# Decoder step on one core: weight splits, two fill pieces and one absorption in another order

## The chip, the cores and the metric

The kernel runs on one core of a Trainium2 chip. The metric is device time in microseconds (us), the median of three runs. In the rows PE is TensorE's matmuls, PEld its weight loads, DVE VectorE, ACT ScalarE, POOL GpSimd and SP SyncE, which issues DMAs.

## What is computed

One inference step of a hybrid decoder with two layers (DEPTH = 2, width 1024) for a prompt of 512 tokens and for 8 samples of one token, which share the weights. Per layer, cut from the reference:

```python
h = RMSNorm(x); z = h @ W_in
# A: gated linear recurrence, 4 heads; B: latent attention, 8 heads, paged cache of 4096;
# C: gated short convolution
x = x + W_out(concat[A (256), B (512), C (256)])
x = x + SwiGLU(RMSNorm(x))          # hidden width 2816 = 22 tiles of 128
```

The arithmetic is float32. A product of two float32 factors is made of three matmuls: each factor is split into a high part, rounded to the engine's fp32r form, and a low part, the difference; the three are high x high, low x high and high x low.

## The kernel before

**Tiles.** Activations lie transposed: `xt[e]`, e = 0 to 7, holds 128 features of all 520 columns (512 prompt and 8 sample tokens), and a column half is 260 wide. A weight tile `wr` of 128 x 1024 comes by DMA; `wh<-wr` on ACT (or a cast on DVE) makes its high part and `wl<-wr,wh` on DVE its low part. For gated weights the names are `wg` and `wu` (raw), `wgh` and `wgl` (parts). All of these are tiles of pool `w`, which has ten slots (NW_SLOTS, L231). A new tile waits until the last reader of the slot's earlier tile is done. The order on each engine is the order of the program text; every engine runs its own queue in order, and a DMA issue stands in the queue of SP or ACT.

**A layer.** First the projections of h (`z_phase`), in the order of the string `ZSEQ` (L69): z0 to z5 are dense products, k0 to k3 and v0 to v3 keys and values, and `A` calls `absorb` (L815). `absorb` multiplies the samples' queries by `wukt` (16 matmuls `qa`) and spreads the rotary part (4 matmuls `bd`), and copies both with DVE (`qabs`, 8 copies `bd`). Its operands `qn` and `qs` are made by POOL, one head after another. `stat` are the matmuls of a norm; they read `sh` and `sl`, the split squares, and behind them come `ra` (DVE), `ry` and `rh` (ACT), `rh` and `kT` (DVE).

Then the mixers, with a loop over the samples' cache chunks. In the last sample's chain PE has little work of its own, and pieces of the first half of the output projection (matmuls `wo`) are laid between its steps: `FILL1` (L59) and `FILL2` say how many pieces at which step. A tile of `wo` has 24 matmuls in pieces of 9, 9 and 6. `mx` is the transposed maximum of the scores, `ml` the low part of the samples' mixed values; half 1 of the projection needs `ml`.

`out_half(1)` (L1531) is the other column half, tiles n = 0 to 7 with e = 7 - n. The first three use weights that were kept, the others the items at+8 to at+12. Within a tile each step of 128 features has its three matmuls (mh x wh, ml x wh, mh x wl) behind each other. After a tile DVE adds it to `xt[e]`, and ACT and DVE make the gain splits `hh`, `hl` and the square `sq` of the tile before.

**Feed-forward network.** `ffn` (L1678) runs a list of jobs: for the hidden tiles 0 to 3 plain ones (`Plain`: gate with `wg`, then up with `wu`, each 48 matmuls), for the others `Seven`, which makes four products out of seven with sums and differences of the operands, and `Down`, which multiplies finished hidden tiles (`fh`, `fl`) by `wd`. `job.load()` issues the DMAs of the gate's and the up half's weights, `prep_all(0)` splits the first, `prep_all(1)` the second. `differences` is a generator of four sets (`re`, `ro`, `t13`, `t24` and their parts) that `Seven` needs; the loop in `ffn` takes two steps of it at each step of a job (L1703), as well as one step of `end_step` (the gate's activation and `fh`, `fl`) and, where due, one `step()` (loads and splits for a later job).

Of the kernel before, what the change touches and what calls it, by code (L numbers as in the profile page):

```python
# [20 lines left out]
S = 512  # L21
# [34 lines left out]
HOFF = (0, 2, 4, 9, 10)  # L56
AOFF = (0, 1, 2, 4, 6, 7, 9)

FILL1 = [1, 1, 1, 1, 1, 1, 0, 1, 1, 0, 1, 1, 1] + [0] * 8 + [0, 1, 0, 1]  # L59
FILL2 = [1, 1, 1, 1, 2, 2, 2]  # L60
LAST = 8
EARLY = 1
# [3 lines left out]
NH = 4  # L66
TFIRST = 7
PREP = 24
ZSEQ = "s Q e1 v0 k0 v1 G0 v2 v3 G1 z2 e0 H k1 z3 k2 A z4 k3 S z5"  # L69
PVW = 2  # L70
PARTS = (3, 3, 3, 3, 3, 3, 4)
PLAIN = (0, 1, 2, 3)
# [156 lines left out]
class Trunk:  # L229
# [1301 lines left out]
    def out_half(self, half):  # L1531
        at = self.at[self.l]['out']
        if half == 0:
            self.ahead = 1
            self.early = EARLY0
            self.limit = at + 16 - KEEP
            self.w_queue = self.nc.scalar
            self.w_dma(at)
            self.w_dma(at + 1)
            self.acts = [(self.t("mh", F32R), self.t("ml", F32R)) for _ in range(8)]  # L1540
            self.kept = {}
            for k in (6, 7, 0, 1, 2, 3, 4, 5):
                c = slice(0, S if 2 <= k < 6 else T)
                self.split(self.acts[k][0][:, c], self.acts[k][1][:, c], self.mixed[k][:, c])
                yield
                if k == 0:
                    self.w_split(at)
                    self.w_dma(at + 2)
                if k == 4:
                    self.w_split(at + 1)  # L1550
            self.prepared = True
            yield
        else:
            self.ahead = AH2
            self.w_queue = self.nc.sync
            self.early = 1
            self.jobs = self.ffn_jobs()
            self.h2 = [None] * 8
            for k in range(2, 6):
                self.split(self.acts[k][0][:, S:T], self.acts[k][1][:, S:T], self.mixed[k][:, S:T])  # L1560
            self.w_split(at + 8)
            self.w_hi(at + 9)
        c = slice(half * CH, (half + 1) * CH)
        for n in range(8):
            e = 7 - n if half else n
            b = self.ps("wo")
            wt = self.kept.pop(e) if half and n < KEEP else self.w_get(at + 8 + n - KEEP if half else at + n)
            if half:
                self.dense(wt, self.acts, 0, 8, {half: b}, 8, (half,))
            else:  # L1570
                for k0, nk in ((0, 3), (3, 3), (6, 2)):
                    self.dense([x[:, k0 * P:(k0 + nk) * P] for x in wt], self.acts, k0, nk, {half: b}, 8, (half,))
                    if k0 < 6:
                        yield
                if n >= 8 - KEEP:
                    self.kept[e] = wt
            del wt
            if half and n:
                self.h2[e + 1] = self.gain_split(e + 1, G_FFN)
                self.square_in(e + 1)  # L1580
            self.tt(self.xt[e][:, c], self.xt[e][:, c], b[:, 0:CH], ALU.add)
            if half:
                if n == 3:
                    self.jobs[0].load()
                if n == 5:
                    self.jobs[0].prep_all(0)
                if n == 6:
                    self.jobs[1].load()
                    self.jobs[0].prep_all(1)
            yield  # L1590
        if half:
            self.h2[0] = self.gain_split(0, G_FFN)
            self.square_in(0)
            self.x_sums()
# [83 lines left out]
    def ffn(self):  # L1678
# [11 lines left out]
        at, loaded = 1, 2  # L1690

        def step():
            nonlocal at, loaded
            at = next(todo, len(jobs))
            while loaded < min(len(jobs), at + 3):
                jobs[loaded].load()
                loaded += 1

        for n, job in enumerate(jobs):
            while at <= n:  # L1700
                step()
            for k, _ in enumerate(job.run()):
                for _ in range(2):  # L1703
                    if extra is not None and self.rstd2 is not None and next(extra, self) is self:
                        extra = None
                self.end_step()
                if at <= n + job.far:
                    step()
                    if job.pace > 1 and at <= n + 1:
                        step()  # L1710
            if not last and len(jobs) - n in (4, 3, 2):
                m = 4 - (len(jobs) - n)
                if m == 0:
                    self.w_dma(nxt)
                    self.w_dma(nxt + 1)
                elif m == 1:
                    self.w_split(nxt)
                    self.w_dma(nxt + 2)
                else:
                    self.w_split(nxt + 1)  # L1720
                    self.w_hi(nxt + 2)
                    self.w_dma(nxt + 3)
            if job.f == FF - 1 and not isinstance(job, Down):
                self.h3 = self.diffs = None
# [290 lines left out]
```

## Time and profile before

| | us |
|---|---|
| median of three runs | 2197.75 (2195.72 to 2198.5) |
| profiled execution, its own time | 2197.29 |
| its span | 2195.2 |
| PE busy in the span | 2147.8 |
| DVE, ACT, POOL busy | 1760.1, 1291.1, 436.6 |
| granted TensorE clock, mean | 0.998 |

Busy time of PE is time with a matmul in its pipeline. The span goes from the first instruction to the last. A row of a timeline has the start and the duration in us; behind it, in brackets, how long the engine stood idle ahead of it and what ended that.

### The profile page before, as it was taken

The numbers are of one execution on the slowest core, as the hardware profiler recorded it, in microseconds if no ns is written. First come the engines' busy times: TensorE is split into PE (matmuls) and PEld (weight loads), VectorE is DVE, ScalarE is ACT, GpSimd is POOL, SyncE is SP. The second block draws the span as 40 slices with busy tenths as digits, with TensorE's granted clock in tenths as the row PEclk, the third lists the DMA queues.
The fourth block names the chain that finished last, engine by engine and source line by source line (L and its number), as shares of the span: only waits on it lengthen the run. The fifth ranks groups of instructions, "written<-read, shape, count | busy, mean of one in ns | idle before, by whom it ended". The sixth has DMA issues, their size and how long they took to land.

```text
span 2195.2 us, 50795 instructions
## 1 busy us (share of the span) xinstructions
PE 2147.8 (98%) x18330; PEld 2013.3 (92%) x18330; DVE 1760.1 (80%) x3673; ACT 1291.1 (59%) x3364; POOL 436.6 (20%) x470
## 2 busy tenths in 40 slices
PE   8999999999999999999999999999999999999999
PEld 8998888888888999999999988888888889999999
DVE  7778889877676699889777788897776857998895
ACT  6667767677674554444356677676776745444341
POOL 0004334333362000000001134234333610000000
PEclk9999999999999999999999999999999999999999
DMA  5213445453574423333233134445445733333232
GB/s 183 99 49 107 116 129 146 129 148 119 165 227 142 136 84 106 106 110 98 77 103 105 59 96 138 124 134 151 135 130 163 237 120 117 110 106 102 90 104 78
DMA packets 149484, 267.72 MB, mean 122 GB/s; under 512 B 22833, under 2 KB 103090, under 8 KB 149234
## 3 DMA queue, kind: packets, MB, share of 16 engines
q1 hardware_dynamic: 121778, 178.47, 25.7%
q0 software_dynamic: 24576, 75.52, 11.9%
q10 hardware_dynamic: 2880, 10.49, 1.5%
q8 instruction: 145, 2.38, 0.4%
q14 instruction: 105, 0.86, 0.1%
HBM read 259.86 MB, written 4.54 MB: 120 GB/s over the span
## 4 chain that ended last, share of the span: by engine, by line
PE 77%; DVE 12%; ACT 7%; issue 3%; DMA 1%; SPq 0%; POOL 0%; DVEq 0%; POOLq 0%; ACTq 0%
PE k L268 29%; PE b L268 17%; PE pr L268 17%; PE pv L268 3%; PE wo L268 3%; ACT ry L283 2%; PE sc L268 2%; DVE ss L1449 1%; DVE wl L271 1%; PE ov L268 1%; DVE ctl L271 1%; PE gr L268 1%; DVE sl L271 1%; ACT wh L283 1%; DVE z L271 1%
## 5 line engine op out<-in xcount | busy, mean ns | idle before, releaser
L268 PE MATMUL k<-wkh,cth 128*128 128x256 f32 (+1 forms) x2048 | 619.7, 303 | 3.4 <-ACT ksq L283 1.9
L268 PE MATMUL k<-wkh,ctl 128*128 128x256 f32 (+1 forms) x2048 | 581.5, 284 | 7.4 <-DVE ctl L271 7.3
L268 PE MATMUL k<-wkl,cth 128*128 128x256 f32 (+1 forms) x2048 | 578.0, 282 | 0.0
L283 ACT ACTIVATE ksq<-k 128x256 f32<-128x256 f32 x1024 | 378.8, 388 | 273.2 <-PE k L268 269.3
L1449 DVE TENSOR_REDUCE ss<-ksq 128x8 f32<-128x512 f32 x512 | 347.6, 681 | 169.4 <-ACT ksq L283 165.9
L268 PEld LDWEIGHTS k<-wkh,cth 128*128 128x128 f32 x2048 | 385.8, 188 | 54.9 <-ACT s L283 27.4
L268 PEld LDWEIGHTS k<-wkh,ctl 128*128 128x128 f32 x2048 | 385.3, 188 | 12.6 <-DVE ctl L271 11.8
L268 PEld LDWEIGHTS k<-wkl,cth 128*128 128x128 f32 x2048 | 386.1, 189 | 6.5 <-issue 3.8
L1335 POOL DMA_INDIRECT nat<-in_cn,idx x224 | 231.2, 1032 | 517.7 <-PE pv L268 389.9
L268 PE MATMUL b<-fh,wd 128*128 128x260 f32 x1408 | 232.0, 282 | 1.1 <-ACT fh L283 1.1
L271 DVE TENSOR_TENSOR ctl<-ct,cth 128x512 fp32r<-128x512 f32 x256 | 175.8, 687 | 27.4 <-ACT cth L283 26.8
L268 PEld LDWEIGHTS b<-fh,wd 128*128 128x128 f32 x1408 | 195.3, 188 | 1.5 <-ACT fh L283 1.5
L283 ACT ACTIVATE swh<-sw 128x512 fp32r<-128x512 f32 x144 | 90.8, 631 | 133.6 <-DVE sw L271 129.7
L283 ACT ACTIVATE cth<-ct 128x512 fp32r<-128x512 f32 x256 | 163.2, 637 | 1.2 <-DMA ct<-in_ct 1.1
L268 PE MATMUL b<-fl,wd 128*128 128x260 f32 x704 | 141.8, 283 | 0.5 <-DVE fl L271 0.5
L1314 POOL DMA_INDIRECT kr<-in_krt,idx x128 | 132.4, 1034 | 38.6 <-issue 36.4
L268 PE MATMUL b<-hh,wh 128*128 128x260 f32 x640 | 130.7, 285 | 8.0 <-ACT wh L283 7.2
L268 PE MATMUL b<-hl,wh 128*128 128x260 f32 x640 | 130.1, 285 | 0.2 <-DVE hl L274 0.2
L268 PE MATMUL b<-hh,wl 128*128 128x260 f32 x640 | 129.8, 284 | 0.0
L271 DVE TENSOR_TENSOR x<-x,b 128x260 f32<-128x260 f32 x224 | 84.8, 420 | 33.5 <-PE b L268 32.4
L268 PEld LDWEIGHTS b<-fl,wd 128*128 128x128 f32 x704 | 108.4, 188 | 0.9 <-DVE fl L271 0.9
L268 PEld LDWEIGHTS b<-hh,wh 128*128 128x128 f32 x640 | 99.7, 190 | 8.7 <-ACT wh L283 7.2
(346 smaller groups left out, 5209.2 us busy)
## 6 DMA issues: line engine op xcount, KB each, us to landing
ct<-in_ct SPq DMA_DIRECT2D x512, 128.0 KB
wg<-in_w_gate SPq DMA_DIRECT2D x44, 512.0 KB
wu<-in_w_up SPq DMA_DIRECT2D x44, 512.0 KB
wr<-in_w_in SPq DMA_DIRECT2D x40, 512.0 KB
wdr<-in_w_down SPq DMA_DIRECT2D x96, 192.0 KB
wr<-in_w_out ACTq DMA_DIRECT2D x20, 512.0 KB
wdr<-in_w_down SPq DMA_DIRECT2D x16, 256.0 KB
nat<-in_cn,idx POOLq DMA_INDIRECT x224, 3.5
```

Of the source, the lines that this page charges most:

```text
L268: self.nc.tensor.matmul(out, lhsT, rhs, start=start, stop=stop)
L271: (e or self.nc.vector).tensor_tensor(out=out, in0=a, in1=b, op=op)
L283: self.nc.scalar.activation(out=out, in_=a, func=f, **k)
L1314: nc.gpsimd.indirect_dma_start(out=k[:, gq * P:(gq + 1) * P], out_offset=None, in_=a['krt'].rearrange("l n c -> (l n) c"), in_offset=bass. ...
L1335: nc.gpsimd.indirect_dma_start(out=nat(b, i)[:, 0:512], out_offset=None, in_=a['cn'].rearrange("l n c -> (l n) c"), in_offset=bass.Indirec ...
L1449: nc.vector.tensor_reduce(out=ss[:, 8 * t:8 * t + 8], in_=sq[:, 0:512].rearrange("p (h d) -> p h d", d=64), axis=AX.X, op=ALU.add)
```

## The change

Four edits. `FILL1` lays two more fill pieces ahead of `mx`, in the fifth and sixth step, and the later pieces move up by as many. `ZSEQ` has `A` between v3 and G1, before z2, and no more behind k2. `out_half(1)` starts with job 0's loads; of the projection's own items it loads at+8 there (it is already split) and takes the high part of at+9 at n = 1; job 0's first weight is split at n = 1 and its second at n = 3, job 1's loads are issued at n = 4 and its first weight is split at n = 6. In `ffn` the steps of `end_step` and `step()` stand ahead of the two steps of `differences`; a branch for jobs of another pace is gone.

```diff
--- before.py
+++ after.py
@@ -56,7 +56,7 @@
 HOFF = (0, 2, 4, 9, 10)
 AOFF = (0, 1, 2, 4, 6, 7, 9)
 
-FILL1 = [1, 1, 1, 1, 1, 1, 0, 1, 1, 0, 1, 1, 1] + [0] * 8 + [0, 1, 0, 1]
+FILL1 = [1, 1, 1, 1, 2, 2, 0, 1, 1, 0, 1, 1, 1] + [0] * 8 + [0, 1, 0, 1]
 FILL2 = [1, 1, 1, 1, 2, 2, 2]
 LAST = 8
 EARLY = 1
@@ -66,7 +66,7 @@
 NH = 4
 TFIRST = 7
 PREP = 24
-ZSEQ = "s Q e1 v0 k0 v1 G0 v2 v3 G1 z2 e0 H k1 z3 k2 A z4 k3 S z5"
+ZSEQ = "s Q e1 v0 k0 v1 G0 v2 v3 A G1 z2 e0 H k1 z3 k2 z4 k3 S z5"
 PVW = 2
 PARTS = (3, 3, 3, 3, 3, 3, 4)
 PLAIN = (0, 1, 2, 3)
@@ -1558,8 +1558,8 @@
             self.h2 = [None] * 8
             for k in range(2, 6):
                 self.split(self.acts[k][0][:, S:T], self.acts[k][1][:, S:T], self.mixed[k][:, S:T])
-            self.w_split(at + 8)
-            self.w_hi(at + 9)
+            self.w_dma(at + 8)
+            self.jobs[0].load()
         c = slice(half * CH, (half + 1) * CH)
         for n in range(8):
             e = 7 - n if half else n
@@ -1580,13 +1580,17 @@
                 self.square_in(e + 1)
             self.tt(self.xt[e][:, c], self.xt[e][:, c], b[:, 0:CH], ALU.add)
             if half:
+                if n == 0:
+                    self.w_split(at + 8)
+                if n == 1:
+                    self.jobs[0].prep_all(0)
+                    self.w_hi(at + 9)
                 if n == 3:
-                    self.jobs[0].load()
-                if n == 5:
-                    self.jobs[0].prep_all(0)
+                    self.jobs[0].prep_all(1)
+                if n == 4:
+                    self.jobs[1].load()
                 if n == 6:
-                    self.jobs[1].load()
-                    self.jobs[0].prep_all(1)
+                    self.jobs[1].prep_all(0)
             yield
         if half:
             self.h2[0] = self.gain_split(0, G_FFN)
@@ -1700,14 +1704,12 @@
             while at <= n:
                 step()
             for k, _ in enumerate(job.run()):
+                self.end_step()
+                if at <= n + job.far:
+                    step()
                 for _ in range(2):
                     if extra is not None and self.rstd2 is not None and next(extra, self) is self:
                         extra = None
-                self.end_step()
-                if at <= n + job.far:
-                    step()
-                    if job.pace > 1 and at <= n + 1:
-                        step()
             if not last and len(jobs) - n in (4, 3, 2):
                 m = 4 - (len(jobs) - n)
                 if m == 0:
```

SP's queue at half 1 of layer 0, before. `wr` are the items at+10, at+11 and at+12 of the output projection, `wg` and `wu` gated weights of job 0, then of job 1.

```order
L374 DMA wr_12995<-in_w_out 128x1024
L374 DMA wr_13001<-in_w_out 128x1024
L374 DMA wr_13005<-in_w_out 128x1024
L1773 DMA wg_13039<-in_w_gate 128x1024
L1773 DMA wu_13040<-in_w_up 128x1024
L1773 DMA wg_13152<-in_w_gate 128x1024
L1773 DMA wu_13153<-in_w_up 128x1024
```

After:

```order
L1775 DMA wg_12900<-in_w_gate 128x1024
L1775 DMA wu_12901<-in_w_up 128x1024
L374 DMA wr_13003<-in_w_out 128x1024
L374 DMA wr_13009<-in_w_out 128x1024
L374 DMA wr_13013<-in_w_out 128x1024
L1775 DMA wg_13088<-in_w_gate 128x1024
L1775 DMA wu_13089<-in_w_up 128x1024
```

Job 0's two loads stand ahead of the three items of the projection now, and their slots with them.

DVE in the same half before, from the first part of x6's row on (`x_81` is x6, `x_80` x5); `wl` are the low parts for tiles 6 and 7.

```order
L274 SCALAR_TENSOR_TENSOR hl_13032<-x_81,gains_74,hh_13031 128x520
L271 TENSOR_TENSOR sq_12989<-sq_12989,sq_13035 128x520
L271 TENSOR_TENSOR x_80<-x_80,wo_12992 128x260
L271 TENSOR_TENSOR wl_13044<-wr_13001,wh_13003 128x1024
L274 SCALAR_TENSOR_TENSOR hl_13073<-x_80,gains_74,hh_13072 128x520
L271 TENSOR_TENSOR sq_12957<-sq_12957,sq_13076 128x520
L271 TENSOR_TENSOR x_79<-x_79,wo_13043 128x260
L271 TENSOR_TENSOR wl_13081<-wr_13005,wh_13046 128x1024
```

After:

```order
L274 SCALAR_TENSOR_TENSOR hl_13040<-x_81,gains_74,hh_13039 128x520
L271 TENSOR_TENSOR sq_12997<-sq_12997,sq_13043 128x520
L271 TENSOR_TENSOR x_80<-x_80,wo_13000 128x260
L271 TENSOR_TENSOR wgl_13049<-wu_12901,wgh_13047 128x1024
L271 TENSOR_TENSOR wl_13052<-wr_13009,wh_13011 128x1024
L274 SCALAR_TENSOR_TENSOR hl_13081<-x_80,gains_74,hh_13080 128x520
L271 TENSOR_TENSOR sq_12959<-sq_12959,sq_13084 128x520
L271 TENSOR_TENSOR x_79<-x_79,wo_13051 128x260
L271 TENSOR_TENSOR wl_13093<-wr_13013,wh_13054 128x1024
```

A `wgl` of job 0 stands ahead of the `wl` of tile 6; before, that `wl` came right behind the add to x5.

DVE in the projections of layer 0 behind v3, before: `wl` and `wh` are weights of z2 and of the next products.

```order
L271 TENSOR_TENSOR wl_1750<-wr_1548,wh_1620 128x1024
L387 CAST wh_1752<-wr_1622 128x1024
L271 TENSOR_TENSOR sl_1786<-sq_1780,sh_1785 128x520
L271 TENSOR_TENSOR wl_1825<-wr_1622,wh_1752 128x1024
L387 CAST wh_1827<-wr_1754 128x1024
L271 TENSOR_TENSOR z_1879<-b_324_1823,rstd_362 128x260
```

After:

```order
L271 TENSOR_TENSOR wl_1750<-wr_1548,wh_1620 128x1024
L387 CAST wh_1752<-wr_1622 128x1024
L271 TENSOR_TENSOR sl_1786<-sq_1780,sh_1785 128x520
L824 COPY qabs_1820<-qa_1821 128x128
L833 COPY bd_1732<-bd_1831 32x8x4 x8
L271 TENSOR_TENSOR wl_1847<-wr_1622,wh_1752 128x1024
L387 CAST wh_1849<-wr_1754 128x1024
L271 TENSOR_TENSOR z_1901<-b_327_1845,rstd_362 128x260
```

The copies of `absorb` stand behind `sl` here; before, they stood behind a later `sl`, that of k2.

## Rows read from the trace of the kernel before

**Rows 1.** The page, part 1: busy time, share of the span, instructions.
```profile
PE 2147.8 (98%) x18330; PEld 2013.3 (92%) x18330; DVE 1760.1 (80%) x3673; ACT 1291.1 (59%) x3364; POOL 436.6 (20%) x470
```

**Rows 2.** PE's waits: engine, line, releaser: us in total, times, longest us.
```profile
PE b L268 <- DVE wgl L271: 3.8, 2, 1.9
```

**Rows 3.** Stretches, layer 0: length; busy us PE, PEld, DVE, ACT, POOL; clock; DMA.
```profile
763.70:767.11 3.41, 3.41 (x18) 3.41 (x17) 3.41 (x7) 2.71 (x4) 0.00 (x0) 0.50 0.10 18
767.12:770.53 3.41, 3.41 (x31) 3.41 (x30) 3.41 (x7) 0.44 (x1) 0.00 (x0) 1.00 0.11 39
757.79:794.25 36.46, 34.56 (x275) 34.25 (x274) 36.31 (x67) 19.09 (x29) 0.00 (x0) 0.95 0.14 41
800.00:850.00 50.00, 50.00 (x419) 50.00 (x418) 49.71 (x114) 23.38 (x41) 0.00 (x0) 1.00 0.33 106
171.40:174.80 3.40, 3.40 (x27) 3.32 (x27) 1.95 (x6) 1.69 (x4) 2.79 (x3) 1.00 0.69 204
```

**Rows 4.** Timeline, feed-forward network: start, duration, engine, instruction, idle before and its releaser.
```profile
754.63 1.06 ACT L283 ACTIVATE wgh<-wu 128x1024 fp32r<-128x1024 f32 x1 [3.90 <-issue]
...
755.59 0.83 ACT L283 ACTIVATE ry<-stat,consts 128x260 f32<-128x260 f32 x2
...
762.89 0.51 PE L268 MATMUL b<-hh,wgl 128*128 128x260 f32 x2 [1.90 <-DVE wgl L271]
...
794.98 0.51 PE L268 MATMUL b<-fh,wd 128*128 128x260 f32 x2 [0.61 <-ACT fh L283]
```

**Rows 5.** Timeline of PE, last chain of layer 0's samples and half 1.
```profile
695.43 0.27 PE L1365 MATMUL mx<-consts,m 128*8 128x128 f32 x1 [1.30 <-DVE m L271]
...
720.17 0.38 PE L268 MATMUL wo<-ml,wh 128*128 128x260 f32 x1 [0.43 <-DVE ml L271]
```

**Rows 6.** Timeline of DVE, the same stretch.
```profile
716.07 0.43 DVE L271 TENSOR_TENSOR x<-x,wo 128x260 f32<-128x260 f32 x1 [1.16 <-PE wo L268]
```

**Rows 7.** Timeline of POOL, PE and DVE, projections of layer 0.
```profile
137.84 1.16 POOL L278 TENSOR_SCALAR qn<-ev,gains 64x8 f32<-64x8 f32 x1
...
153.97 1.85 PE L268 MATMUL qa<-qn,wukt 128*128 128x16 f32 x16
...
156.12 0.48 PE L268 MATMUL b<-hh,wh 128*128 128x260 f32 x2
...
160.12 0.69 DVE L271 TENSOR_TENSOR sl<-sq,sh 128x520 fp32r<-128x520 f32 x1
...
160.94 1.20 DVE L833 COPY bd<-bd 32x32 f32<-32x32 f32 x8
...
162.07 0.28 PE L268 MATMUL stat<-sl,mats 128*128 128x260 f32 x1
...
171.37 0.39 PE L268 MATMUL stat<-sl,mats 128*128 128x260 f32 x1 [1.47 <-DVE sl L271]
```

**Rows 8.** Timeline of PE, SP, ACT and DVE, half 1 of layer 0.
```profile
728.07 0.28 PE L268 MATMUL wo<-mh,wh 128*128 128x260 f32 x1
...
728.19 0.33 SPq L374 DMA_DIRECT2D wr<-in_w_out  x1
...
728.61 2.35 DVE L271 TENSOR_TENSOR wl<-wr,wh 128x1024 fp32r<-128x1024 f32 x2
...
730.95 0.28 PE L268 MATMUL wo<-mh,wh 128*128 128x260 f32 x1
...
731.70 1.06 ACT L283 ACTIVATE wh<-wr 128x1024 fp32r<-128x1024 f32 x1 [3.65 <-DMA wr<-in_w_out]
...
732.67 0.71 ACT L283 ACTIVATE hh<-x,gains 128x520 fp32r<-128x520 f32 x1
...
733.29 0.62 ACT L283 ACTIVATE sq<-x 128x520 f32<-128x520 f32 x1
...
733.42 0.76 DVE L274 SCALAR_TENSOR_TENSOR hl<-x,gains,hh 128x520 fp32r<-128x520 f32 x1 [2.46 <-ACT hh L283]
...
734.10 0.69 DVE L271 TENSOR_TENSOR sq<-sq,sq 128x520 f32<-128x520 f32 x1
```

## The prediction

> **What bounds the kernel now.** I read the page first: of a span of 2195.2 us PE is busy 2147.8 us [rows 1], so 47 us is all that an order can win. PE is the bound; what counts is where it stands still and what ends that. In the list of PE's waits the second factors `wgl` of the gated weights stand with 3.8 us in two waits, one in each layer [rows 2]. The timelines show the place in layer 0, and layer 1 repeats it. The wait of 1.90 costs more than itself: behind it the granted clock is 0.50 for 3.41 us, in which 18 matmuls run where the next 3.41 us hold 31. That is 13 matmuls at 0.12 us, about 1.5 us [rows 3, 4]. And from 757.79 to 794.25 DVE is busy 36.31 of 36.46 us [rows 3]: DVE, not PE, sets when `fh` comes, and PE waits 0.61 for it at 794.98 although it had lost 1.90 and 1.5 us just before [rows 4].
>
> The profiled execution took 2197.29 us, 0.46 below the median of 2197.75. I sum on its rows and add the sum to the median.
>
> **Fill pieces: -1.7 us per layer.** Two more pieces are 18 matmuls of 0.12 us, 2.2 us of work ahead of `mx`, where PE now stands 1.30 us for DVE's `m` [rows 5]. They cover the wait and put `mx` some 0.7 us later. Their weights are needed one piece earlier, and `p` comes at about the time PE asks for it; from there PE has 18 matmuls fewer to do before half 1. So `ml` must come earlier too, or its wait of 0.43 grows [rows 5]. It can: `ra` now stands behind an add that waits for PE's tile [rows 6], and the changed order puts `ra` ahead of it. The add still needs 24 matmuls after `stat`, 2.9 us, and `ml` follows it. I count both waits, 1.30 and 0.43, as gone. If `ml` is late by 0.7 the gain is 1.0; nothing else is there to win, so 1.0 to 1.7.
>
> **Absorption of the queries: +1.2 us per layer.** The 16 `qa` and 4 `bd` matmuls hold PE for 2.15 us, from 153.97 to 156.12, and the copies hold DVE for 1.4 [rows 7]. At the new place, which PE reaches at 138.0, the last pair of `qn` is not there: POOL ends it at 139.0 [rows 7]. PE gets through 6 of the 16 and waits 0.45. At the old place this work was cover. DVE's chain from one `stat` to the next `sl` ended at 160.81, and PE came for it at 162.07: 1.26 us of slack [rows 7]. Without 2.15 us of PE work in that stretch PE comes 0.9 too early. Behind that `sl` DVE goes to `wl`, `z` and `ra` without the copies, so the chain to the next `sl`, for which PE waits 1.47 at 171.37, takes 1.4 us less. Added up: the first `sl` ends 2.6 us later (2.15 moved ahead of it, 0.45 waited), the next one 2.6 - 1.4 = 1.2 later, and PE's `stat` with it. With `qn` in time it would be +0.75; 0 if PE's shift is taken up at once. Bounds 0 to 1.4.
>
> **Half 1 of the output projection: +4.85 us per layer.** PE has no wait here: a tile of 24 matmuls starts every 2.88 us [rows 8]. The change loads job 0's two weights at the start, into two of the ten slots of pool w, and splits the first at n = 1, the second at n = 3. The loads of the last three tiles' weights (at+10 to at+12) stand behind these in SP's queue, and the slots that they take come free one tile later than before: in the built order at+11, the weights of tile 6, waits for the end of tile 3, at+12 for that of tile 4. Let S be the start of tile 4. The load is issued at S + 0.1; the one issued at 728.19 had landed when `wh` began at 731.70, 3.5 us on [rows 8]. So `wh` of tile 6 holds ACT from S + 3.65 to 4.7. Behind it on ACT, in order, stand `hh` (0.71) and `sq` (0.62) of x6 and job 0's second `wgh` (1.04): to S + 5.4, 6.0 and 7.05. DVE, in order, does `hl` of x6 (0.68 from start to start), the sum of `sq` (0.61), an add to x5 (0.35), then job 0's second `wgl`, held by that `wgh` to S + 7.05 and 1.13 long [rows 8], and only then `wl` of tile 6: S + 8.2 to 9.4. PE asks for that `wl` at the third matmul of tile 6, S + 5.75 + 0.25 = 6.0, and waits 3.45 us. The floor of this term is in the slots: `wl` of tile 6 takes the slot that tile 5 leaves at S + 5.7, so even with DVE free PE waits 1.0.
>
> Tile 6 then ends at S + 12.1. `wl` of tile 7 takes a slot that tile 6 leaves and runs 1.22 us from there: PE waits 0.95. By then the gain splits of x4 to x1 are late on DVE, with job 1's first `wgl` now among them, and `hl` of x1 comes about 0.4 us after PE asks for it in the last eighth of job 0's gate. Together 3.45 + 0.95 + 0.4, and 0.05 at tile 5: 4.85. Bounds 2.4 (the two slot waits and 0.4) and 5.5.
>
> **Clock behind that wait: +1.5 us per layer.** The rows show a half clock behind the wait of 1.90 and full clock behind that of 1.47 [rows 3]. A wait of 3.45 is longer than the one that cost the clock, so I count one such stretch. Bounds 0 and 3.0 (two stretches).
>
> **Feed-forward part: -0.55 us per layer, and +1.5 for the clock.** Let U be the end of job 0's second half on PE, 754.6 [rows 4]. Job 1's first factor is split before U and its second right behind it, so the wait of 1.90 and the half clock go, 3.6 us with the restart. But `fh` of the first down job is late next. `ra` now stands behind that `wgl`, so ACT's `ry` starts 1.6 after U, not 0.96 [rows 4]: the chain to `rstd` is 0.6 later. Behind it DVE has one `wgl` of 1.13 less. It runs without a gap there, and weights ahead of differences take no difference out from before this `gt`. So `gt`, and with it `fh`, comes 0.55 earlier after U, while PE, 3.6 us earlier, waits 3.7 us in place of 0.61. By the rows on the clock a half clock follows, and nothing behind takes that loss up: from 800 to 850 PE is busy 50.00 of 50 us [rows 3]. Bounds -1.1 to -0.3, and 0 to 1.5.
>
> **Sum.** Per layer -1.7 + 1.2 + 4.85 + 1.5 - 0.55 + 1.5 = 6.8 us; two layers 13.6; 2197.75 + 13.6 = 2211.
>
> The Trainium skill, DMA: Bandwidth & Descriptors, "Rules for kernel authors", tells authors to issue a DMA early, compute, and wait on its semaphore late, so that the fixed cost is hidden. By that rule job 0's early loads cost nothing, which is the second rival; the row of 3.5 us from issue to use bears it out, but the rule does not count the slot that an early load holds.
>
> **Rivals.** First, the splits in half 1 wait for their slots alone: loads land sooner or DVE catches up, and PE waits 1.0 + 0.95 + 0.4 with no clock lost; `fh` still costs 1.5. Per layer -1.7 + 1.2 + 2.4 - 0.55 + 1.5 = 2.85: 2203.5. For it: the floor follows from the order. Against it: `wgh`, `wgl` and `wl` stand in one line on two engines behind a load of measured length.
>
> Second, half 1 stays free of waits because the early loads fit: -1.7 + 1.2 - 0.55 + 1.5 = 0.45 per layer, 2198.6, no change. Against it: tile 5 must leave its slot before `wl` of tile 6 is written, and PE asks 0.3 us later.
>
> Third, faster: weights ahead of differences let the `gt` of the first down job overtake. If DVE ends it 3.1 us earlier than I count, PE keeps 3.6 us and the clock; with the slot waits alone in half 1 and the absorption at its bound of 0 that is -1.7 + 2.4 - 3.6 = -2.9 per layer, 2192.0. It decides at the point where three operand splits (0.6 each) and one pair of `re` and `ro` (1.35) fall behind that `gt`. Against it: the built order has all four sets of differences begun ahead of it.
>
> Fourth, the change does not do what its pieces say: `ml` follows `mx`, the fill wins nothing, and the forecast grows by 3.4 to 2214.5.
>
> **Chances.** Forecast, with the clock lost at one or both places and the fourth rival in it (2206 to 2217): 0.62. First rival, 2200 to 2206: 0.16. Second: 0.11. Third: 0.11. A difference under about 0.2% (4.4 us) can't be told from no change on this kernel, so faster is below 2193.4 and slower above 2202.1. Slower is the 0.62 and most of the first rival, 0.74; same 0.14, the second and the low end of the first; faster 0.12. The range leaves out the third rival and the far ends: 2198 to 2217.
>
> **What would show it.** Right: PE waits over 2 us for DVE's `wl` at tile 6 of half 1 and about 1 at tile 7; a granted clock of 0.50 behind that; no wait for `wgl`; 3 to 4 us for `fh`; none at `mx`; 0.45 at `qa`, then `stat` waits of about 0.9 and 1.4. Wrong: half 1 without waits, so that my reading of the slots fails, or a wait for `fh` under 1 us, so that DVE was not the bound.

## The result, and the profile after

The changed kernel takes 2214.5 us (median of 6 runs, 2211.9 to 2215.2), the kernel before on the same chip 2197.6. The ratio is 1.0073 with a 95% interval of 1.0063 to 1.0084: slower by 16.9 us in the medians, 2214.5 where 2211 was forecast with a range of 2198 to 2217. The profiled execution has a span of 2211.5 us and an own time of 2213.2.

The page, part 1, of the changed kernel, to be read beside [rows 1]: PE is busy 6.4 us longer, with the same number of matmuls; 20.5 us of its span stand at half clock around its waits (below), where 6.8 stood before. The rest of the longer span is waiting.

```profile
PE 2154.2 (97%) x18330; PEld 2018.5 (91%) x18330; DVE 1760.8 (80%) x3673; ACT 1291.4 (58%) x3364; POOL 435.6 (20%) x470
```

PE's waits in the changed kernel: engine, line, releaser: us in total, times, longest us.

```profile
PE b L268 <- ACT fh L283: 9.8, 2, 4.9
PE wo L268 <- DVE wl L271: 8.0, 5, 3.2
...
PE mx L1365 <- DVE m L271: 1.4, 4, 0.4
```

Before, the wait for `wgl` stood in this list with 3.8 us [rows 2]. It is gone. In its place stand 9.8 us for `fh`, one wait in each layer, where 1.1 stood before, and 8.0 for `wl` in half 1, where no wait was.

The timeline of half 1 in layer 0, SP, ACT, DVE and PE: start, duration, engine, instruction, and in brackets the idle time ahead and its releaser. It answers to [rows 8].

```profile
729.34 0.33 SPq L374 DMA_DIRECT2D wr<-in_w_out  x1
...
732.95 1.06 ACT L283 ACTIVATE wh<-wr 128x1024 fp32r<-128x1024 f32 x1 [1.71 <-DMA wr<-in_w_out]
733.91 0.71 ACT L283 ACTIVATE hh<-x,gains 128x520 fp32r<-128x520 f32 x1
734.53 0.62 ACT L283 ACTIVATE sq<-x 128x520 f32<-128x520 f32 x1
735.06 1.04 ACT L283 ACTIVATE wgh<-wu 128x1024 fp32r<-128x1024 f32 x1
...
736.28 1.22 DVE L271 TENSOR_TENSOR wgl<-wu,wgh 128x1024 fp32r<-128x1024 f32 x1
737.42 1.22 DVE L271 TENSOR_TENSOR wl<-wr,wh 128x1024 fp32r<-128x1024 f32 x1
...
738.69 0.39 PE L268 MATMUL wo<-mh,wl 128*128 128x260 f32 x1 [2.99 <-DVE wl L271]
...
744.32 0.39 PE L268 MATMUL wo<-mh,wl 128*128 128x260 f32 x1 [0.97 <-DVE wl L271]
```

This is the line that the prediction wrote down: the load for tile 6 is issued at 729.34, its `wh` starts 3.61 us later, `hh`, `sq` and `wgh` of job 0 stand behind it on ACT, `wgl` and only then `wl` on DVE. PE stands 2.99 us in tile 6 and 0.97 in tile 7.

Stretches of the changed kernel, as in [rows 3]: length; busy us of PE, PEld, DVE, ACT, POOL; granted clock; DMA share and GB/s.

```profile
739.03:742.45 3.42, 3.42 (x18) 3.42 (x17) 1.23 (x3) 1.25 (x2) 0.00 (x0) 0.50 0.74 272
...
800.48:803.89 3.41, 3.21 (x13) 2.99 (x14) 3.13 (x8) 1.49 (x4) 0.00 (x0) 0.50 0.13 11
1834.72:1841.53 6.81, 5.57 (x24) 5.26 (x24) 3.42 (x5) 1.92 (x4) 0.00 (x0) 0.50 0.42 154
1896.16:1902.97 6.81, 4.49 (x19) 4.26 (x20) 6.30 (x15) 3.26 (x7) 0.00 (x0) 0.50 0.19 58
```

At the `wl` wait and at the `fh` wait TensorE's granted clock falls to 0.50, its level of 1.2 GHz, for 3.41 us in layer 0 and for 6.8 us in layer 1. In layer 1 it falls while PE still stands, 1.2 us before the end of the `wl` wait and 2.3 us before the end of the `fh` wait, so part of each long stretch has no matmul to slow down.

### The profile page after: what moved, and what is told of

Read it like the earlier page. It is cut to its first block, busy times and chain, and to the rows that moved or that the text cites. A ratio compares the mean times of both kernels' runs of the same rounds, so it can differ in the third digit from the quotient of the medians.

```text
span 2211.5 us, 50789 instructions
## 1 busy us (share of the span) xinstructions
PE 2154.2 (97%) x18330; PEld 2018.5 (91%) x18330; DVE 1760.8 (80%) x3673; ACT 1291.4 (58%) x3364; POOL 435.6 (20%) x470
## 5 line engine op out<-in xcount | busy, mean ns | idle before, releaser
L271 DVE TENSOR_TENSOR wl<-wr,wh 128x1024 fp32r<-128x1024 f32 (+1 forms) x84 | 91.5, 1091 | 20.0 <-ACT wh L283 13.5
```

The source lines that it names most:

```text
L271: (e or self.nc.vector).tensor_tensor(out=out, in0=a, in1=b, op=op)
```

## Where the 16 us lie

The table takes the start of the same matmul in both profiles and gives what each stretch grew by, in us; the forecast is for one layer. The stretches run from the last of the mixers' values `v` to the first scores `sc` (absorption), from there to job 0's gate (fill pieces, half 1 and its clock), to the gate's first `stat`, to the end of the `fh` wait, and to the first `v` of the next layer or the last matmul.

| stretch | forecast | layer 0 | layer 1 |
|---|---|---|---|
| absorption | +1.2 | +0.3 | +0.3 |
| fill, half 1, its clock | -1.7 + 4.85 + 1.5 = +4.65 | +4.8 | +6.2 |
| gate to `stat` | 0 | +0.3 | +0.2 |
| `stat` to the end of the `fh` wait | -0.55 | +0.75 | +0.75 |
| behind `fh` | +1.5 | +1.25 | +1.9 |
| sum | +6.8 | +7.5 | +9.2 |

The two layers add up to 16.7 us; the changed kernel's profile reaches the first of these matmuls 0.5 us sooner, and its span is 16.3 us longer. The forecast's 0.4 for `hl` of x1 is counted in the second row and falls into the third. The third row can't be put down to the change: in a second execution of the kernel before (below) the same stretch is 0.4 and 0.2 us longer than in the first.

## The experiments

Three chips were used. The runs with one edit each ran on a chip on which the kernel before takes 2197.5 us; the second weight loaded and split late, one step in the old order, the kernel before once more and the last run on one on which it takes 2197.6. The other four (the second split late, one slot more, weights first, one step of differences) ran on a chip on which it takes 2300.6 us: there PE waits 19 to 28 us for `ksq` in front of `k` in the cache chunks, where it waits 1.9 us in the profile of the kernel before. Of those four only ratios to the kernel before on that chip, and stretches behind the mixers, are used.

### One edit at a time

**The fill pieces alone.**

```diff
-FILL1 = [1, 1, 1, 1, 1, 1, 0, ...
+FILL1 = [1, 1, 1, 1, 2, 2, 0, ...
```

> The kernel before with the two fill pieces alone. Theory (the fill's term stands by itself): PE's wait of 1.30 at mx goes and that of 0.43 at ml falls to 0.2 or less, both layers: 2197.6 - 3.1 = 2194.5, ratio 0.9986. Rival (ml follows mx, and what the fill wins comes back as a wait at ml): no change, 2197.6. In between, a part that comes back inside half 1: 2196.

Measured: 2195.5 us, ratio 0.9991 (0.9982 to 1.0000): -2.0 us, not -3.1. The waits at `mx` and `ml` are as the theory says (1.30 gone, `ml` 0.2). From the last `mx` to job 0's gate PE needs 2.1 us less in layer 0 and 1.7 in layer 1, and `mx` comes 0.7 to 0.8 later, so 1.4 and 1.0 are won at the gate. In layer 0 all of it was given back behind that. The timeline of PE in this run, feed-forward part of layer 0, to be read beside [rows 4]:

```profile
760.88 0.50 PE L268 MATMUL b<-hh,wgl 128*128 128x260 f32 x2 [1.87 <-DVE wgl L271]
...
792.97 0.50 PE L268 MATMUL b<-fh,wd 128*128 128x260 f32 x2 [2.11 <-ACT fh L283]
```

Stretches of the same run, with the granted clock in the column behind POOL:

```profile
760.85:764.26 3.41, 3.38 (x28) 3.38 (x29) 3.41 (x8) 2.52 (x4) 0.00 (x0) 1.00 0.00 0
763.70:767.11 3.41, 3.41 (x31) 3.41 (x31) 3.41 (x6) 1.37 (x2) 0.00 (x0) 1.00 0.20 58
793.84:797.25 3.41, 3.41 (x17) 3.41 (x18) 3.31 (x9) 1.53 (x3) 0.00 (x0) 0.50 0.38 105
```

Behind a `wgl` wait of 1.87 the clock stayed full here. PE therefore came to `fh` 1.5 us sooner, but DVE did not: the `fh` wait is 2.11 instead of 0.61, and the half clock stands behind that wait now. In the kernel before the half clock fell where PE would have had to wait for `fh` in any case, so it cost nothing. Here it costs. At the gate and at the end of the `fh` wait this run is 2.0 us ahead of the kernel before, 0.6 of it from the very start of the profile; at layer 1's first `v` only 0.45 is left. In layer 1 the half clock stands where it did before, and 1.0 us is kept.

**The absorption alone.**

```diff
-ZSEQ = "s Q e1 v0 k0 v1 G0 v2 v3 G1 z2 e0 H k1 z3 k2 A z4 k3 S z5"
+ZSEQ = "s Q e1 v0 k0 v1 G0 v2 v3 A G1 z2 e0 H k1 z3 k2 z4 k3 S z5"
```

> The kernel before with the queries' absorption moved and nothing else. Theory 1 (the prediction's term): a wait of 0.45 at qa for qn, waits of 0.9 and 1.4 at the two stat: +1.2 per layer, 2200.0. Theory 2 (DVE's chain has slack of its own that takes up most of the shift): no wait at qa, stat waits of 0.85 and 1.0, +0.3 per layer, 2198.2.

Measured: 2199.5 us, ratio 1.0009 (1.0000 to 1.0018): +2.0 us. By the total theory 1 is right, by the place it is wrong. No wait at `qa`, `stat` waits of 0.87 and 1.00, and `sc` comes 0.33 later in layer 0 and 0.7 in layer 1. The rest is the same shift of the half clock as above, now in layer 1: there the clock stayed full behind a `wgl` wait of 1.91, and PE's next wait in this run's timeline is

```profile
1884.98 0.51 PE L268 MATMUL b<-fh,wd 128*128 128x260 f32 x2 [2.16 <-ACT fh L283]
```

with a granted clock of 0.50 for 3.41 us from 1886.85 on. A single number that agrees with a theory would have hidden this.

**Half 1 alone** (the whole hunk of `out_half`):

```diff
-            self.w_split(at + 8)
-            self.w_hi(at + 9)
+            self.w_dma(at + 8)
+            self.jobs[0].load()
...
+                if n == 3:
+                    self.jobs[0].prep_all(1)
...
```

> The kernel before with the new half 1 of the output projection (early loads and splits of the gated weights) and nothing else. Theory 1 (this half alone makes the loss, the fh wait behind it too): wl waits of about 3 and 1 us in tiles 6 and 7, one half-clock stretch behind them in layer 0 and two in layer 1, no wgl wait, and fh waits of 4 to 5 us with a half clock: +19 us, 2216.5. Theory 2 (the new order in the feed-forward part makes the fh wait longer): the same wl waits, but fh waits of 3 to 3.7 us: +16 us or less, 2213.5.

Measured: 2211.0 us, ratio 1.0059 (1.0045 to 1.0073): +13.5 us. PE's waits in this run:

```profile
PE b L268 <- ACT fh L283: 8.0, 2, 4.0
PE wo L268 <- DVE wl L271: 7.8, 5, 3.1
```

From the last `mx` to the gate PE needs 7.0 us more in layer 0 and 6.2 in layer 1, clock included; the profiled execution took 2214.2 us, 3.2 above the median of five, with a mean granted clock of 0.995 where the other four have 0.997 or 0.998, so these two figures are at the high end. The `fh` waits are 4.03 and 3.94 us, shorter than the 4.88 of the full change, but longer than the 3 to 3.7 of theory 2, whose time it has. From job 0's `stat` to the end of the `fh` wait this kernel is even 0.3 us faster than the kernel before.

**The feed-forward order alone.**

```diff
+                self.end_step()
+                if at <= n + job.far:
+                    step()
                 for _ in range(2):
...
-                self.end_step()
-                if at <= n + job.far:
-                    step()
...
```

> The kernel before with weights ahead of differences in the feed-forward loop and nothing else. Theory 1 (the order moves nothing that PE waits for): wgl wait 1.9 and fh wait 0.6 as before, 2197.6. Theory 2 (the high parts of differences stand behind weights on ACT, DVE waits for them, and gt comes later): fh wait 1.5 to 2.5 in each layer, +2 to +4 us with the clock kept, 2200 to 2202. Theory 3 (the order was needed for gt to overtake): no fh wait, -1.2, 2196.4.

Measured: 2202.3 us, ratio 1.0021 (1.0012 to 1.0031): +4.85 us. Theory 2 is right that DVE waits for a high part of the differences on ACT; it has the size of the `fh` wait wrong and, as the rows and the run with weights first below show, what stands ahead on ACT. The `wgl` wait is down to 0.2, with this edit alone, and the `fh` wait is 4.75 in both layers, with a half clock of 6.8 us that begins 2.4 and 1.7 us before the wait is over. The timeline of ACT, DVE and PE in this run, layer 0:

```profile
781.84 0.64 ACT L283 ACTIVATE fh<-gt 128x520 fp32r<-128x520 f32 x1 [3.74 <-DVE gt L271]
782.38 0.51 ACT L283 ACTIVATE wd<-wdr 128x384 fp32r<-128x384 f32 x1
782.80 0.62 ACT L283 ACTIVATE t13h<-t 128x520 fp32r<-128x520 f32 x1
...
783.45 0.70 DVE L271 TENSOR_TENSOR t13l<-t,t13h 128x520 fp32r<-128x520 f32 x1 [1.04 <-ACT t13h L283]
...
794.59 0.80 PE L268 MATMUL b<-fh,wd 128*128 128x260 f32 x2 [4.75 <-ACT fh L283]
```

ACT's `fh` of an earlier hidden tile waits for DVE's product `gt`, and `t13h` stands behind it. DVE needs `t13h` next and is idle for 1.04 us, in a stretch where it has no other gap. From job 0's `stat` to the end of the `fh` wait this run takes 45.4 us, the kernel before 44.4, and the same in layer 1. The changed kernel has the same row, at 789.74 and with 1.04 us.

The four edits give -2.0, +2.0, +13.5 and +4.85, in sum +18.3 against +16.9 together: additive within the intervals, which are 2 to 3 us to either side for each run. A sum above the whole would fit that half 1 and the feed-forward order both remove the same `wgl` wait and pay for the same `fh`, but these runs do not show it.

### What makes half 1 wait

**The second split late.**

```diff
-                if n == 3:
-                    self.jobs[0].prep_all(1)
...
                 if n == 6:
+                    self.jobs[0].prep_all(1)
                     self.jobs[1].prep_all(0)
```

> The changed kernel with job 0's second weight split at n = 6, as before, and not at n = 3; its early loads, the first split at n = 1 and job 1's first split stay. Theory 1 (wgh and wgl of that split stand ahead of wl of tile 6, and the slot that the second split takes keeps wl of tile 6 waiting for tile 5): wh of tile 6 ends at S + 4.7, S being the start of tile 4, and wl at S + 5.9, where PE asks at S + 6.0: waits of 0 to 0.3 at tiles 6 and 7, no half clock there; the fh wait of 4.9 stays: 2214.5 - 2 x (4.0 + 1.5 to 3) = 2200.5 to 2203.5. Theory 2 (the late load of tile 6 alone is enough, whatever stands behind it): wl waits of 2 to 3 us stay, 2212 or more.

Measured: 1.0033 (1.0016 to 1.0050) of the kernel before on its chip. Tile 7's wait is gone, tile 6 still waits 2.04 us in layer 0 and 1.62 in layer 1, with the clock full behind both. So neither theory: about half of the wait was the second split. PE now waits 0.8 us for `hh` in job 0's gate, where the changed kernel has no such wait. The timeline of DVE in this run shows what was forgotten:

```profile
783.25 0.76 DVE L274 SCALAR_TENSOR_TENSOR hl<-x,gains,hh 128x520 fp32r<-128x520 f32 x1 [2.35 <-ACT hh L283]
783.93 0.69 DVE L271 TENSOR_TENSOR sq<-sq,sq 128x520 f32<-128x520 f32 x1
784.54 0.42 DVE L271 TENSOR_TENSOR x<-x,wo 128x260 f32<-128x260 f32 x1
784.87 1.22 DVE L271 TENSOR_TENSOR wl<-wr,wh 128x1024 fp32r<-128x1024 f32 x1
```

`wh` of tile 6 was ready at 782.6, but `wl` starts at 784.87. ACT makes `hh` of x6 only behind that late `wh`, and DVE has `hl`, `sq` and the add ahead of `wl`: a late load delays work that has nothing to do with it.

**One slot more.**

```diff
-    NT_SLOTS = 68
-    NW_SLOTS = 10
+    NT_SLOTS = 66
+    NW_SLOTS = 11
```

> The changed kernel with eleven slots for weights instead of ten, and 66 instead of 68 for the smaller tiles, to make room; nothing else. In its order the load for tile 6 waits for a split that is over by tile 2 and not for the end of tile 3. Theory 1 (the slot that the early loads hold makes the load of tile 6 late): no wait over 0.3 us in half 1 and no half clock there, 2200.5 to 2203.5. Theory 2 (the line of wgh, wgl and wl on two engines is the cause by itself): the wl wait of tile 6 stays over 1 us, 2206 or more. If fewer small tiles cost something elsewhere, waits for slots show in other places.

Measured: 1.0085 (1.0059 to 1.0111). The total says little, since two small tiles fewer may cost elsewhere and no run with those alone was made. In half 1, tile 7's wait is gone and tile 6 waits

```profile
789.60 0.38 PE L268 MATMUL wo<-mh,wl 128*128 128x260 f32 x1 [2.37 <-DVE wl L271]
```

with a half clock at it in both layers. By the number that is theory 2, but the run is no clean test: the load for tile 6 is issued only 1.1 us earlier than in the changed kernel (9.7 us behind the first matmul with `ml`, not 10.8), while the expectation had it wait for nothing later than tile 2. The slot, too, is only a part as far as this run goes; a load as early as that was not tried.

**The second weight loaded and split late.**

```diff
-            self.jobs[0].load()
+            self.jobs[0].load_half(0)
...
                 if n == 3:
-                    self.jobs[0].prep_all(1)
+                    self.jobs[0].load_half(1)
...
                 if n == 6:
+                    self.jobs[0].prep_all(1)
                     self.jobs[1].prep_all(0)
...
```

`load_half(0)` issues the first of the two loads, `load_half(1)` the second.

> The changed kernel with two things of job 0's second weight as late as before: it is loaded at n = 3 and split at n = 6. Its first weight keeps the early load and split. Each of the two runs before took away one half of the cause (the second split in front of wl, or the slot) and left a wl wait of 2.0 and 2.4 us. Theory 1 (the two halves add up, and nothing else is there): the load for tile 6 is issued some 1.2 us before tile 3 ends, wl of tile 6 ends at S + 6.1, S being the start of tile 4, and PE asks at S + 6.0: no wl wait over 0.4, no half clock in half 1. The fh wait of 4.9 stays. Against the changed kernel -2 x (4.0 + 1.5 to 3): 0.995 of it, 1.002 to 1.003 of the kernel before. Theory 2 (a third cause holds tile 6): a wl wait of 1.5 or more stays.

Measured: 2206.8 us, ratio 1.0041 (1.0026 to 1.0057), 7.7 us less than the changed kernel. Between the theories: a `wl` wait of 1.15 us stays in layer 0 and 1.26 in layer 1, with no half clock in half 1. PE's timeline of this run, half 1 and the gate behind it:

```profile
736.97 0.39 PE L268 MATMUL wo<-mh,wl 128*128 128x260 f32 x1 [1.15 <-DVE wl L271]
...
748.49 0.51 PE L268 MATMUL b<-hh,wgh 128*128 128x260 f32 x2 [0.71 <-ACT hh L283]
```

The second of these waits, for `hh` in the gate, is in neither kernel. The loads for tiles 5, 6 and 7 are issued 6.8, 9.7 and 10.9 us behind the first matmul with `ml`. In the kernel before it is 2.3, 8.0 and 9.7 us, in the changed kernel 8.0, 10.8 and 13.8. So the first weight, with one load and one split ahead, still holds the projection's loads back: the one for tile 5 by 4.5 us. In layer 0 the waits for `wl` go down in steps, 2.99 + 0.97, then 2.04 without the second split, 1.15 without its load. What remains would then belong to the first weight's early load and split, or to job 1's earlier loads, which this run keeps too. Neither was taken away alone, so this last part is not shown; the kernel before, without all of it, has no `wl` wait.

### What sets `fh`

**Weights first, the gate's step last.**

```diff
+                if at <= n + job.far:
+                    step()
                 for _ in range(2):
...
                 self.end_step()
-                if at <= n + job.far:
-                    step()
...
```

> The kernel before with the feed-forward loop alone changed, but in another way than the change does it: the step of the weights first, then the two steps of differences, then the gate's step. Theory 1 (the gate's step ahead of the differences is what costs: ACT's fh, which waits for DVE's product, stands ahead of t13h, and DVE waits 1.04 us for t13h): that DVE wait goes, fh comes 1 us earlier than with the change's order, PE waits 3.7 for it instead of 4.75, and the time is 2202.3 - 2 = 2200.3. Theory 2 (weights ahead of differences are what costs): the fh wait stays at 4.7, 2202.

Measured: 0.9999 (0.9984 to 1.0015) of the kernel before on its chip. PE's timeline of this run:

```profile
840.81 0.80 PE L268 MATMUL b<-fh,wd 128*128 128x260 f32 x2 [3.69 <-ACT fh L283]
```

3.69 us, and 3.77 in layer 1, where the change's order has 4.75: theory 1. DVE's gap at `t13l` is gone, and from `stat` to the end of the `fh` wait PE takes 44.3 us (44.4 in the kernel before), against 45.4 with the change's order. So weights ahead of differences cost nothing; the gate's step ahead of them does.

**One step of differences at a turn**, with the fill and the order of the last run:

```diff
-                for _ in range(2):
+                for _ in range(1):
```

> The kernel before with the two fill pieces, the feed-forward loop in the order weights, differences, gate, and one step of differences at each turn instead of two. So one of four sets of differences, some 5 us of DVE's work, falls behind the gt of the third hidden tile. Theory 1 (DVE sets when fh comes): no wgl wait, no fh wait over 0.5, no half clock, 1.9 + 0.6 + 1.5 us won in each layer beside the fill: 2195.5 - 8 = 2187.5. Rival (DVE has no room behind fh either, and the set comes too late for the first of the seven-product jobs): the wait comes back there, 2195.

Measured: 0.9954 (0.9938 to 0.9970) of the kernel before on its chip, 9 to 11 us of 2300.6, where theory 1 says 10. No `wgl` wait over 0.2, no `fh` wait at all. The rival is right in part. The next wait is at the first of the seven-product jobs, 2.00 us in layer 0 and 1.93 in layer 1, the second with a half clock:

```profile
860.41 0.39 PE L268 MATMUL pr<-reh,wgl 128*128 128x260 f32 x1 [2.00 <-DVE wgl L271]
```

**The same in the old order**, with the fill:

> The kernel before with the two fill pieces and one step of differences at each turn instead of two, in the old order (differences, gate, weights). Theory 1 (two separate causes: wgl of job 1 late because it stands behind steps of differences and ra, fh late because DVE is full): the fh wait is gone as in the run with the new order, the wgl wait of 1.9 stays at 1.2 to 1.9, and its half clock is no longer hidden by the fh wait; 1.0025 to 1.003 of the run with the weights first, 0.998 of the kernel before. Theory 2 (fewer differences free wgl too): no wgl wait, as fast as with the weights first, 0.9955.

Measured: 2193.6 us, ratio 0.9981 (0.9972 to 0.9990): theory 1. The `fh` wait is gone, the `wgl` waits stay at 1.53 and 1.55 us, with the clock full behind them, and those in front of the seven-product job at 1.73 and 1.81, with a half clock. The timeline of PE in this run, layer 0:

```profile
760.79 0.51 PE L268 MATMUL b<-hh,wgl 128*128 128x260 f32 x2 [1.53 <-DVE wgl L271]
...
808.61 0.39 PE L268 MATMUL pr<-reh,wgl 128*128 128x260 f32 x1 [1.73 <-DVE wgl L271]
```

The two causes are separate, but what they are worth does not add up one by one: the fill alone won 2.0 us, weights first alone none, the fill and one step in the old order 4.0, and all three together 9 to 11, each against the kernel before on its own chip. Either edit of the feed-forward loop leaves a wait for DVE in place; only both together take the two away. The profiled execution took 2196.3 us, 2.7 above the median of eleven. In four of the eleven the mean granted clock is 1.000, where one stretch of 3.41 us at half clock would make it 0.999: those executions had no half clock behind either wait.

**The kernel before once more.**

> The kernel before, unchanged: a second profiled execution, beside the others of this chip. Theory 1 (whether a wait of 1.9 us costs the half clock is chance from one execution to the next): wgl waits of 1.9 in both layers as in the first profile, with a half-clock stretch behind one of them only or behind none, and where it is missing an fh wait of about 2.1 instead of 0.6. Theory 2 (it is fixed by the program): a half clock behind both again and fh waits of 0.6.

Measured: 2197.4 us, `wgl` waits of 1.90 and 1.89, a half clock behind both, `fh` waits of 0.6: theory 2. Whether a wait of 1.9 us costs the clock was the same in two executions of one kernel, and differs between kernels in which it is as long. The run above shows that it is not fixed by the program everywhere. The second execution also waits for `hl` in job 0's gate, which the first does not:

```profile
747.87 0.50 PE L268 MATMUL b<-hl,wgh 128*128 128x260 f32 x2 [0.29 <-DVE hl L274]
```

**Better than both kernels**: the run with one step, and in a seven-product job `wgl` made ahead of the sums that are needed later.

```diff
         self.got[4] = uh, ul
+        gl = k.w("wgl", F32R)
+        k.tt(gl[:, 0:D], g[:, 0:D], gh[:, 0:D].bitcast(F32), ALU.subtract)
+        self.got[1] = gh[:, e], gl[:, e]
+        self.got[2] = gh[:, o], gl[:, o]
         yield
...
-        gl = k.w("wgl", F32R)
-        k.tt(gl[:, 0:D], g[:, 0:D], gh[:, 0:D].bitcast(F32), ALU.subtract)
         del g
-        self.got[1] = gh[:, e], gl[:, e]
-        self.got[2] = gh[:, o], gl[:, o]
...
```

> The run with the fill, weights first and one step of differences, and on top the low part wgl of a seven-product job made two steps earlier, since PE's next wait there was 2.0 us for that wgl in front of the first seven-product job. Theory (that wgl stands behind sums and splits that are needed later): the wait falls to 0.4 or less in both layers, and with it 1.6 us each and the half clock behind it in one of them: 0.993 to 0.9945 of the kernel before, against 0.9954 without it. Rival (DVE is full until there, the low parts sl are late next): the same wait moves to sl, 0.9954.

Measured: 2185.0 us, ratio 0.9948 (0.9934 to 0.9961), just above what was expected and 29 us below the changed kernel. The wait in front of the seven-product job is gone in both layers. By the ratios it can't be told from the run without this last step (0.9954), which was on another chip; it is 8.6 us faster than the run in the old order, on the same chip. From 750 to 850 us the stretches of this run, of the kernel before and of the changed kernel read

```profile
750.00:850.00 100.00, 99.81 (x832) 99.61 (x831) 94.08 (x198) 50.91 (x86) 0.00 (x0) 1.00 0.30 92
```

```profile
750.00:850.00 100.00, 97.26 (x794) 96.63 (x794) 93.36 (x195) 49.99 (x83) 0.00 (x0) 0.98 0.27 89
```

```profile
750.00:850.00 100.00, 94.84 (x775) 94.16 (x774) 89.04 (x184) 48.95 (x80) 0.00 (x0) 0.98 0.29 92
```

PE gets through 832 matmuls in this stretch, then 794, then 775. DVE's sum of work was not too much: DVE is busier here than in either kernel. What stood ahead of what PE needs next was the loss.

## Why the prediction was right, and which steps were off

**What bounds.** Right: PE is the bound, and in the feed-forward part DVE sets when `fh` comes. The change removed 1.90 us of waiting and a half clock in each layer and got neither back. Both stood ahead of a wait for DVE, so PE only waits there instead, 4.88 us in place of 0.61, and the half clock moves behind the wait, where nothing takes it up.

**Fill, -1.7 forecast.** Right in mechanism and at the optimistic end in size: alone it wins 1.4 and 1.0 at the gate, and 2.0 us in all where 3.4 were forecast. In the changed kernel PE's rows, beside [rows 5], are

```profile
696.09 0.27 PE L1365 MATMUL mx<-consts,m 128*8 128x128 f32 x1
...
718.52 0.39 PE L268 MATMUL wo<-ml,wh 128*128 128x260 f32 x1 [0.20 <-DVE ml L271]
```

`mx` without a wait and 0.7 later, as said; of the 0.43 at `ml` 0.20 remains.

**Absorption, +1.2 forecast, +0.3 measured.** The failed step is the wait of 0.45 at `qa`. PE's and POOL's rows of the changed kernel, beside [rows 7]:

```profile
137.31 1.16 POOL L278 TENSOR_SCALAR qn<-ev,gains 64x8 f32<-64x8 f32 x1
...
137.52 1.85 PE L268 MATMUL qa<-qn,wukt 128*128 128x16 f32 x16
...
162.21 0.39 PE L268 MATMUL stat<-sl,mats 128*128 128x260 f32 x1 [0.85 <-DVE sl L271]
...
171.16 0.39 PE L268 MATMUL stat<-sl,mats 128*128 128x260 f32 x1 [0.99 <-DVE sl L271]
```

POOL ends `qn` at 138.47, 1.2 us behind the start of the last `v`, as reckoned. But only the last quarter of the 16 reads it, and it starts at about 138.8; I had PE stop behind the sixth. That leaves the +0.75 that the text gives for `qn` in time. The other 0.4 went into DVE's chain, which had a wait of 0.53 us for ACT's `rh` at 147.63 before and shows none now. The first `stat` wait is 0.85 where 0.9 was forecast, the second 0.99 where 1.4 was.

**Half 1, +4.85 and 1.5 for the clock.** Right in both waits: 2.99 + 0.97 us in layer 0 and 3.15 + 0.67, with 0.18 at tile 5, in layer 1, where 3.45 + 0.95 + 0.05 were forecast. The 0.4 for `hl` of x1 is not borne out as a cost of the edit: the changed kernel waits 0.28 there, and the kernel before waits 0.29 in its second execution. Alone the edit costs 7.0 and 6.2 us, in an execution 3.2 us above the median, where the two terms give 6.35. The clock was priced at one stretch a layer; it was one or two. The text puts the floor into the slots of tiles 5 and 6 and the rest into the line behind the second split. The experiments bear out that the line counts (2.04 us are left without the second split) and that the early loads count (1.15 are left without the second weight's load), and add what the text does not have: with the second split gone, `hh`, `hl`, `sq` and an add still stand between `wh` and `wl`, and the first weight holds the load for tile 5.

The second rival rested on the rule to issue early and wait late (the Trainium skill, DMA: Bandwidth & Descriptors, "Rules for kernel authors"). PE has no wait for a `wgh` or `wgl` of job 0 at its gate, before or after the change, so nothing here speaks against the rule for the moved load itself. The loads that were pushed back pay: tile 6's is issued 10.8 us behind the first matmul with `ml` instead of 8.0.

**Feed-forward part, -0.55 forecast, +0.75 measured.** The wrong sign. The failed step is the sentence on the order: DVE "runs without a gap there", and weights ahead of differences take nothing out from before `gt`. The second half is true, as the run with the gate's step last shows (0.1 us less than before). But the edit also puts the gate's step ahead, and I gave that no price, since it adds no work. It costs DVE a gap of 1.04 us, because ACT's `fh` waits for DVE and holds `t13h`. What was said on the early split of job 1 holds in part: half 1 alone brings `fh` 0.3 earlier after `stat`, where 0.55 was forecast; with the gap that gives the +0.75. I put the end of the `wgl` wait down to half 1; the order alone ends it as well.

**Clock behind `fh`, +1.5, bounds 0 to 1.5.** 1.25 us in layer 0 and 1.9 in layer 1. The bound was too low: the half clock lasted 6.8 us in layer 1.

**The sum.** 13.6 forecast, 16.9 measured. Absorption was 0.9 a layer too dear; the order of the gate's step (1.3 a layer) and the second stretches of half clock in layer 1 more than made up for it. That the sum lies near the measured time is in part luck, since these errors point in different directions. All four rivals fall: the slots were not the only wait in half 1 (first), half 1 is not free (second), `gt` did not overtake (third), and the fill does win (fourth). The fourth rival's time, 2214.5, is the measured one, but by chance: its ground, a fill that wins nothing, does not hold.

## What to carry to other kernels

A wait that stands ahead of another engine's bound can't be won by removing it: follow the engine that sets the next wait, and take work from in front of that (weights earlier won nothing by itself; with one step of differences at a turn and the two fill pieces the same order won 10 us). Price such edits together, since each alone can leave the next wait in place. In queues that run in order, an instruction that waits costs what stands behind it, even when it adds no work; look for the one that waits for the engine that waits for its neighbour. An early load is paid by the loads whose slots it takes, and a late load by everything queued behind its first consumer.

## What the runs showed of the hardware

The granted clock at a wait of PE, in the ten profiles from the chips where the kernel before takes 2197 us, PE's first wait of the program aside: full behind all waits up to 1.65 us; behind the `wgl` waits of 1.87 to 1.91 us half in six cases of eight, one kernel giving the same twice; half behind 1.73 and 1.81 us; and half at every wait from 2.1 to 4.9 us, for 3.41 or 6.8 us. On the third chip waits of 2.00 and 2.04 us left it full and one of 1.93 did not. So the length of the wait alone does not decide it near 1.9 us, and neither does the program: the kernel with the waits of 1.73 and 1.81 us has a mean granted clock of 1.000 in four executions of eleven, so no half clock there, while its profiled one has it behind both. What else decides was not found. In the half-clock rows 18 matmuls run where 31 run at full clock, and whether that costs anything depends on what PE waits for next.
